# Reading a 64 MiB input at another row pitch: seven blocks at 448 KiB and one at 64 KiB, in place of eight at 512 KiB

## The chip, the cores and the metric

The kernel runs on one core of a Trainium2 chip. The metric is the time of one execution on the device in microseconds (us), as the median of several runs. All runs told of here are fast (granted clock 1.000, nothing disturbed). The input lies in HBM, the chip's main memory; DMA engines copy it in packets to the on-chip memory, whose 128 rows are called partitions. A transfer has *landed* when all its packets have arrived and the waiting engine may go on. The span that a profile shows is 1.7 to 1.8 us shorter than the time of the same run.

## The reference

```python
x = np.random.randn(32, 512, 1024).astype(np.float32)      # 64 MiB
multiplier = 0.5
def reference(x, multiplier):
    return (np.sum(x, axis=-1) * multiplier).astype(np.float32)   # [32, 512]
```

There are 16384 rows of 1024 numbers (4 KiB each). Each row becomes one number, and no row depends on another: any row may lie on any partition, as long as its sum is stored in the right place.

## The kernel before

The 16384 rows are dealt to 128 partitions, 128 consecutive rows each. A block is 16 rows of every partition (8 MiB), there are eight blocks, and three buffers. Seven blocks are loaded by one DMA each and split between two engines: VectorE reduces eight rows by one instruction, ScalarE takes eight by one activation each.

```python
x_flat = x.flatten_outer_dims()
N, D = x_flat.shape
rows = N // P                                   # 128 rows per partition
x_rows = x_flat.rearrange("(p c) d -> p c d", p=P)
out_view = out.rearrange("b s -> (b s)").rearrange("(p c) -> p c", p=P)
B = 16
n_blocks = rows // B                            # 8
x_pool = ctx.enter_context(tc.tile_pool(name="x", bufs=3))
# ... (cut)
for b in range(n_blocks - 1):
    c0 = b * B
    t = x_pool.tile([P, B, D], fp32, name="xb")
    loads.append(nc.sync.dma_start(out=t, in_=x_rows[:, c0 : c0 + B, :]))
    h = B // 2
    nc.vector.reduce_sum(out=sums[:, c0 : c0 + h], in_=t[:, 0:h, :], axis=mybir.AxisListType.X)
    # ... (cut: the multiplication by 0.5)
    for r in range(h, B):
        act_row(t, r, c0 + r)                   # ScalarE, one row of all partitions
# ... (cut) the last block comes in five DMAs, of 8, 5, 2 rows, 640 and 384 columns of the last row,
# so that little is left to compute after the last of them; its sums go out by a store of their own
nc.sync.dma_start(out=out_view[:, 0:c1], in_=res[:, 0:c1])        # 56 KB
# ... (cut)
store = nc.sync.dma_start(out=out_view[:, c1:], in_=res[:, c1:])  # 8 KB, the end of the kernel
```

A step from one partition to the next is 128 rows in HBM: a pitch of 512 KiB, for all eight blocks.

## Time and profile before

| | |
|---|---|
| time | 162.91 us (162.87 to 163.31, 3 runs) |
| span of the profiled run | 160.9 us |
| share of the DMA queue in 16 engines' span | 97.2% |
| VectorE, ScalarE busy | 42%, 42% |
| a steady packet of x (64 KiB, one partition's 16 rows) | 2.418 us |
| landing of the last piece of x but one, on which the chain waits | 157.43 us, taken up at 157.46 us |
| landing of the last piece (192 KB) | 157.91 us |

These lines are from the page of the kernel before: the span, the busy tenths of the DMA engines in 40 slices, the DMA queues (packets, MB, share of 16 engines), the chain that ended last by engine, and the two costliest groups (busy us and mean ns of one; then idle us before them and what ended it).

```profile
span 160.9 us, 236 instructions
...
DMA  7997997998998998998998998998998998999991
...
q1 hardware_dynamic: 2016, 67.18, 97.2%
q14 instruction: 1, 0.01, 0.0%
...
DMA 86%; DVE 11%; SPq 1%; issue 0%; DVEq 0%
...
L50 ACT ACTIVATE xb<-xb 128x1024 f32<-128x1024 f32 x63 | 65.6, 1043 | 88.2 <-DMA xb<-in_x_dram 88.2
L76 DVE TENSOR_REDUCE sums<-xb 128x8 f32<-128x8192 f32 x7 | 60.8, 8686 | 85.0 <-DMA xb<-in_x_dram 85.0
```

Both computing engines stand idle for more than half of the span, nearly all of it waiting for x. The one queue of loads and stores keeps the 16 engines busy for 97.2% of the span.

The next lines are the stage table of the kernel before: stretch in us, its length, busy time of the engines, then clock, DMA share and GB/s.

```profile
core 0: us, DVE busy (x) ACT busy (x) POOL busy (x), PEclk, DMA share, GB/s
22.00:41.50 19.50, 8.86 (x2) 8.42 (x16) 0.00 (x0) 1.00 0.99 430
41.50:60.90 19.40, 8.86 (x2) 8.42 (x16) 0.00 (x0) 1.00 1.00 432
...
80.20:99.60 19.40, 8.86 (x2) 8.42 (x16) 0.00 (x0) 1.00 1.00 433
```

And these are pieces of its chain of waits (start, length, what). The pieces between them are a wait for a buffer (a VectorE reduction) and issues.

```profile
0.43 41.13 DMA xb<-in_x_dram
...
50.36 49.27 DMA xb<-in_x_dram
...
109.78 47.66 DMA xb<-in_x_dram
...
157.46 0.49 DVE xb L60
...
158.04 0.42 DVE xb L60
```

The DMA share is 0.99 to 1.00 while blocks stream in. The chain steps over a reduction of 8.7 us twice only because a load waits there for its buffer; two more blocks are queued at that time, so the engines don't run dry. From 157.46 us, when the last piece but one has landed, two short VectorE operations and a store remain, 3.4 us in all; the last piece lands during the first of them. (The prediction's "last landing" is the 157.46 us.)

Last, the start of the first five reductions on VectorE, from the timeline (start, length, ..., idle before and what ended it). Each starts when its block has landed on all partitions, so this is a clock of the load stream.

```profile
22.26 8.69 DVE L76 TENSOR_REDUCE sums<-xb 128x8 f32<-128x8192 f32 x1 [22.26 <-DMA xb<-in_x_dram]
41.59 8.69 DVE L76 TENSOR_REDUCE sums<-xb 128x8 f32<-128x8192 f32 x1 [10.43 <-DMA xb<-in_x_dram]
60.94 8.69 DVE L76 TENSOR_REDUCE sums<-xb 128x8 f32<-128x8192 f32 x1 [10.46 <-DMA xb<-in_x_dram]
80.29 8.69 DVE L76 TENSOR_REDUCE sums<-xb 128x8 f32<-128x8192 f32 x1 [10.46 <-DMA xb<-in_x_dram]
99.65 8.69 DVE L76 TENSOR_REDUCE sums<-xb 128x8 f32<-128x8192 f32 x1 [10.47 <-DMA xb<-in_x_dram]
```

A block takes 19.33 to 19.36 us: eight packets of 2.42 us on each engine. The first one comes at 22.26 us.

### The profile page before, as it was taken

What the parts mean: (1) busy time and instruction counts of PE and PEld (TensorE: products, weight loads), DVE (VectorE), ACT (ScalarE), POOL (GpSimd) and SP (SyncE); (2) the same over time, 40 slices, a digit from 0 to 9 for tenths busy, and PEclk for the clock granted to TensorE, in tenths of its full rate; (3) what the DMA queues carried; (4) which work ended last, traced back from release to release, by engine and by line L of the source; (5) the groups of instructions that cost most, each with busy time, mean ns of one, the idle gap of its engine ahead of it and who ended that gap; (6) DMA issues with size and microseconds to landing.
All of it is one profiled execution on the core that took longest, in us unless ns stands there. A gap on an engine that the chain in (4) does not pass through costs nothing.

```text
span 160.9 us, 236 instructions
## 1 busy us (share of the span) xinstructions
DVE 68.1 (42%) x34; ACT 67.8 (42%) x127; POOL 0.2 (0%) x4
## 2 busy tenths in 40 slices
DVE  0000049700695008930099102990049700597453
ACT  3000049600694008920099001980039700596952
POOL 0000000000000000000000000000000000000000
DMA  7997997998998998998998998998998998999991
GB/s 261 522 440 342 522 440 342 522 424 359 522 424 359 522 424 359 522 424 359 522 424 361 522 407 375 522 407 375 522 407 375 522 407 375 407 448 396 425 386 40
DMA packets 2017, 67.18 MB, mean 418 GB/s; under 512 B 480, under 2 KB 608, under 8 KB 736
## 3 DMA queue, kind: packets, MB, share of 16 engines
q1 hardware_dynamic: 2016, 67.18, 97.2%
q14 instruction: 1, 0.01, 0.0%
HBM read 67.11 MB, written 0.07 MB: 418 GB/s over the span
## 4 chain that ended last, share of the span: by engine, by line
DMA 86%; DVE 11%; SPq 1%; issue 0%; DVEq 0%
DMA xb<-in_x_dram 86%; DVE sums L76 11%; SPq L94 1%; DVE xb L60 1%; SPq L74 0%; DVE part L60 0%; DVEq L190 0%
## 5 line engine op out<-in xcount | busy, mean ns | idle before, releaser
L50 ACT ACTIVATE xb<-xb 128x1024 f32<-128x1024 f32 x63 | 65.6, 1043 | 88.2 <-DMA xb<-in_x_dram 88.2
L76 DVE TENSOR_REDUCE sums<-xb 128x8 f32<-128x8192 f32 x7 | 60.8, 8686 | 85.0 <-DMA xb<-in_x_dram 85.0
L50 ACT ACTIVATION_READ_ACCUMULATOR xb<-xb 128x1 f32 x63 | 11.8, 187 | 0.0
L60 DVE CUSTOM_DVE_ANT_0 xb<-xb 128x512 f32<-128x512 f32 (+1 forms) x9 | 5.6, 667 | 5.1 <-DMA xb<-in_x_dram 4.9
L50 ACT ACT_TABLE_LOAD x1 | 1.3, 1283 | 1.7 <-PEq L176 1.7
L79 DVE TENSOR_SCALAR res<-sums 128x8 f32<-128x8 f32 x7 | 1.2, 172 | 0.2
L60 DVE DVE_READ_ACCUMULATOR2_ANT res<- 128x1 f32 x9 | 0.7, 83 | 0.0
L60 DVE CUSTOM_DVE_ANT_0 xb<-xb,part 128x192 f32<-128x192 f32 x1 | 0.4, 419 | 0.1
L176 POOL MEMSET const-uint8-127<- 128x1 uint8 x1 | 0.1, 103 | 0.0
L176 POOL MEMSET const-bfloat16-1.0<- 128x1 bf16 x1 | 0.1, 102 | 0.0
L176 POOL MEMSET const-float32-0.0<- 128x1 f32 x1 | 0.1, 99 | 0.2 <-issue 0.2
L176 POOL MEMSET const-float32-1.0<- 128x1 f32 x1 | 0.1, 99 | 0.0
L60 DVE DVE_READ_ACCUMULATOR2_ANT part<- 128x1 f32 x1 | 0.1, 83 | 0.0
## 6 DMA issues: line engine op xcount, KB each, us to landing
xb<-in_x_dram SPq DMA_DIRECT2D x1, 4096.0 KB, 39.6
xb<-in_x_dram SPq DMA_DIRECT2D x1, 2560.0 KB, 45.4
xb<-in_x_dram SPq DMA_DIRECT2D x1, 1024.0 KB, 47.4
xb<-in_x_dram SPq DMA_DIRECT2D x1, 320.0 KB, 47.7
xb<-in_x_dram SPq DMA_DIRECT2D x1, 192.0 KB, 47.6
xb<-in_x_dram SPq DMA_DIRECT2D x7, 49.3
out_dram<-res SPq DMA_DIRECT2D x1, 56.0 KB, 10.8
out_dram<-res SPq DMA_DIRECT2D x1, 8.0 KB, 1.4
```

Source lines behind the costliest of these rows:

```text
L50: acts.append(nc.scalar.activation(out=t[:, r, :], in_=t[:, r, :], func=mybir.ActivationFunctionType.Copy, scale=mul, accum_out=res[:, col ...
L60: nc.vector.tensor_tensor_reduce(out=t[:, r, lo:mid], in0=t[:, r, lo:mid], in1=t[:, r, mid:hi], scale=mul, scalar=start, op0=ADD, op1=ADD, ...
L76: nc.vector.reduce_sum(out=sums[:, c0 : c0 + h], in_=t[:, 0:h, :], axis=mybir.AxisListType.X)
L79: nc.vector.tensor_single_scalar(out=res[:, c0 : c0 + h], in_=sums[:, c0 : c0 + h], scalar=mul, op=mybir.AluOpType.mult,)
L94: nc.sync.dma_start(out=t[:, lo:hi, :], in_=x_rows[:, c0 + lo : c0 + hi, :])
L176: nc = _bacc.Bacc("TRN2", target_bir_lowering=False, num_devices=1)
```

## The change

The intent: take the large power of two out of the addresses that the 128 partitions read side by side. Seven blocks form one region in which a partition's rows are 112 rows apart (448 KiB); the last block forms a region of its own, 16 rows apart (64 KiB, so the 8 MiB are contiguous). The sums of each region then are contiguous in the output too.

```diff
-    x_rows = x_flat.rearrange("(p c) d -> p c d", p=P)
-    out_view = out.rearrange("b s -> (b s)").rearrange("(p c) -> p c", p=P)
+    out_flat = out.rearrange("b s -> (b s)")
...
+    own = rows - B                              # 112
+    x_rows = x_flat[0 : P * own, :].rearrange("(p c) d -> p c d", p=P)
+    x_last = x_flat[P * own : N, :].rearrange("(p c) d -> p c d", p=P)
+    out_rows = out_flat[0 : P * own].rearrange("(p c) -> p c", p=P)
+    out_last = out_flat[P * own : N].rearrange("(p c) -> p c", p=P)
...   # the five loads of the last block
-                out=t[:, lo:hi, :], in_=x_rows[:, c0 + lo : c0 + hi, :]
+                out=t[:, lo:hi, :], in_=x_last[:, lo:hi, :]
...
-    nc.sync.dma_start(out=out_view[:, 0:c1], in_=res[:, 0:c1])
+    nc.sync.dma_start(out=out_rows, in_=res[:, 0:own])
...
-    store = nc.sync.dma_start(out=out_view[:, c1:], in_=res[:, c1:])
+    store = nc.sync.dma_start(out=out_last, in_=res[:, own:])
```

The instructions on all engines are the same in number, order and shape; only addresses in HBM differ.

More of the change, by code (lines that the diff above doesn't have):

```diff
@@ L100 @@
             nc.sync.dma_start(
-                out=t[:, B - 1, lo:hi], in_=x_rows[:, c0 + B - 1, lo:hi]
+                out=t[:, B - 1, lo:hi], in_=x_last[:, B - 1, lo:hi]
             )
         )
-    c1 = c0
-    nc.sync.dma_start(out=out_view[:, 0:c1], in_=res[:, 0:c1])
+    nc.sync.dma_start(out=out_rows, in_=res[:, 0:own])
     on_act = {4, 5, 6, 7, 11, 12, 14}
```

## The prediction

> **What bounds the kernel.** The transfers from HBM, and not by HBM but by the 16 DMA engines themselves. The page gives the hardware queue 97.2% of 16 engines' span; VectorE and ScalarE are busy 42% each and wait for x (groups of instructions: 85.0 us and 88.2 us of idle time, released by the DMA). The chain of waits is 86% DMA of x. Its 11% of `sums` reduction is only the wait of a buffer's next load, while two blocks are already queued: the stage table shows the DMA share at 0.99 to 1.00 from 22 to 119 us (430 to 435 GB/s). So everything up to the last landing at 157.5 us is the load stream; the remaining 3.4 us are two short VectorE operations, the last 8 KB store (1.4 us to landing) and the end.
>
> **The packet records.** A packet is 64 KiB, one partition's 16 rows. In the steady part nearly every one takes 2.418 to 2.420 us (27.1 GB/s per engine, 434 GB/s for 16), without spread. The Trainium skill, "DMA: Bandwidth & Descriptors", section Bandwidth, puts the ceiling of the 16 SBUF ports at 435.2 GB/s; the trace agrees within 0.5%. The same page, section Latency and other measured facts, gives 207 GB/s at a row pitch of 512 KiB against 214 for a padded pitch, in copies from HBM to HBM. This trace shows no such loss: at 512 KiB the engines already run at their ceiling.
>
> **What the change does.** Nothing is removed or added: same 12 loads, two stores, bytes, tiles and engine work. Seven blocks are read at a pitch of 448 KiB in place of 512 KiB, the last at 64 KiB, each still as contiguous runs of 64 KiB.
> - Steady packets: no gain; 64 packets' worth per engine at 2.42 us stay 154.8 us.
> - First block: its packets have a mean of 2.515 us against 2.420; the excess is 8 x 0.095 = about 0.8 us per engine, nearly all in each engine's first packet (3.0 to 3.5 us). I take it for the fill of the stream; were it pitch conflicts, 0.8 us is the most that could come back. I allow 0.1 us.
> - First store (56 KB): runs of 448 B, now adjacent instead of 512 B apart; its packets (25 ns, eight per engine) end the stream beside the computing. Nothing.
> - Last store, on the critical path: 128 runs of 64 B, 512 B apart before, adjacent now (8 KB contiguous). If runs merge, or neighbouring partial writes collide, its 1.4 us may move by 0.2 us either way.
>
> **Prediction: 162.8 us**, 8 in 10 from 162.2 to 163.5. Faster by over 2%: 0.02; within 2%: 0.96; slower by over 2%: 0.02.
>
> **What would show it.** Right: steady packets stay at 2.42 us, last landing of x at 157 to 158 us, same order of waits, tail of 3.2 to 3.6 us. Conflicts that matter: first-block packets near 2.42 us and the last landing 0.5 us or more earlier. A bad new pitch: packets over 2.5 us in the first seven blocks (448 KiB) or only in the last (64 KiB), and the DMA share below 1.00 or GB/s below 430 in those stages.
>
> **What would make it wrong.** Several of the 16 engines meeting in one part of HBM at one of the new pitches, so that it and not the engine sets the packet's time; fewer engines for the now contiguous stores; or sessions that differ by more than the 0.3% seen in three runs.

## The result, and the profile after

| | before | after |
|---|---|---|
| time, median (lowest to highest) | 163.01 us (162.87 to 163.31, 6 runs) | 162.59 us (162.52 to 162.73, 6 runs) |
| ratio, 95% interval | | 0.9973 (0.9960 to 0.9986) |

A ratio here is the mean time of one kernel's fast runs over the mean of the other's fast runs of the same rounds, so it isn't quite the ratio of the medians. The time is inside the predicted range and within 2%, as predicted. But the two sets of runs don't overlap: there is a small gain, 0.42 us between the medians, where 0.1 us had been allowed for. The range is 1.3 us wide, three times the gain, so that the time alone says little about the reasoning behind it. The six runs of before were also 0.1 us slower in the median than the 162.91 us from which the prediction was reckoned, and this hides a part of the miss.

The lines of the page, the stage table and the chain of the kernel after, as above:

```profile
span 160.8 us, 236 instructions
...
DMA  7996996996996996996996996996996996998990
...
q1 hardware_dynamic: 2016, 67.18, 97.3%
q14 instruction: 1, 0.01, 0.0%
...
DMA 86%; DVE 11%; SPq 1%; issue 0%; DVEq 0%
...
L55 ACT ACTIVATE xb<-xb 128x1024 f32<-128x1024 f32 x63 | 65.6, 1042 | 88.2 <-DMA xb<-in_x_dram 88.2
L81 DVE TENSOR_REDUCE sums<-xb 128x8 f32<-128x8192 f32 x7 | 60.8, 8686 | 85.0 <-DMA xb<-in_x_dram 85.0
```

```profile
core 0: us, DVE busy (x) ACT busy (x) POOL busy (x), PEclk, DMA share, GB/s
22.00:41.50 19.50, 9.01 (x3) 8.57 (x17) 0.00 (x0) 1.00 0.99 430
41.50:60.90 19.40, 8.91 (x3) 8.47 (x17) 0.00 (x0) 1.00 1.00 432
...
80.20:99.60 19.40, 8.62 (x2) 8.28 (x16) 0.00 (x0) 1.00 1.00 433
```

```profile
0.43 40.80 DMA xb<-in_x_dram
...
50.03 49.57 DMA xb<-in_x_dram
...
109.71 47.74 DMA xb<-in_x_dram
...
157.47 0.49 DVE xb L65
...
158.02 0.42 DVE xb L65
```

Nothing has moved: the stages have the same GB/s, and the last piece of x but one is taken up at 157.47 us in place of 157.46 (the last lands at 157.89 in place of 157.91). The profiled run of before took 162.63 us, less than any of its six timed runs, and so these two profiles can't show the gain by their ends. The clock of the load stream says more (start of the first five reductions, after):

```profile
21.91 8.69 DVE L81 TENSOR_REDUCE sums<-xb 128x8 f32<-128x8192 f32 x1 [21.91 <-DMA xb<-in_x_dram]
41.26 8.69 DVE L81 TENSOR_REDUCE sums<-xb 128x8 f32<-128x8192 f32 x1 [10.46 <-DMA xb<-in_x_dram]
60.61 8.69 DVE L81 TENSOR_REDUCE sums<-xb 128x8 f32<-128x8192 f32 x1 [10.46 <-DMA xb<-in_x_dram]
79.97 8.69 DVE L81 TENSOR_REDUCE sums<-xb 128x8 f32<-128x8192 f32 x1 [10.46 <-DMA xb<-in_x_dram]
99.62 8.69 DVE L81 TENSOR_REDUCE sums<-xb 128x8 f32<-128x8192 f32 x1 [10.77 <-DMA xb<-in_x_dram]
```

After is 0.35 us ahead at the first block (21.91 against 22.26), and keeps 0.32 to 0.35 us until the fourth. Then it loses them in one step: from the fourth to the fifth block it takes 19.65 us, before 19.36. The records of single packets name both steps. They are no view of the page, so they are given here in words and as a table worked out from them. (A record doesn't name its engine; a packet is counted to the engine whose packet ends where it starts.)

```
                                                      before     after
start of the 16 engines' first packets, us        1.01..1.91   1.00..1.55   (mean 1.38 / 1.13)
first packets, mean duration, us                       3.18         3.20
end of the first packets, mean (latest), us      4.56 (4.99)  4.33 (4.65)
later 64 KiB packets, starting after 5 us: mean       2.4203       2.4202
packet of the instruction queue: start, length  86.40, 0.31  83.97, 0.31
x packet just behind it: start, length          86.70, 2.72  84.28, 2.78
last engine done with block 4 / block 5, us     79.90, 99.23  79.51, 99.14
```

(Block 4 and block 5 count from one.) In both kernels one DMA engine has to fetch 8 KiB of instructions in between. That takes 0.31 us, and the engine's next packet takes 2.72 or 2.78 us by the record instead of 2.42: in sum it falls behind by 0.61 us in before and 0.67 us in after. In the profiled run of before this engine had been 0.75 us ahead of the last one and stayed 0.14 us ahead of it, so the last landing didn't move. In the profiled run of after it had been only 0.37 us ahead, and became the last one by 0.30 us. So the theory to test: the new pitch lets the engines start earlier, by a quarter of a microsecond on average and more for the latest of them; and the fetch took nearly all of it back in this pair of profiles.

### The profile page after: what moved, and what is told of

The parts are those of the page before. It is cut to its first block, busy times and chain, and to the rows that moved or that the text cites. A ratio compares the mean times of both kernels' runs of the same rounds, so it can differ in the third digit from the quotient of the medians.

```text
span 160.8 us, 236 instructions
## 1 busy us (share of the span) xinstructions
DVE 68.1 (42%) x34; ACT 67.9 (42%) x127; POOL 0.2 (0%) x4
## 4 chain that ended last, share of the span: by engine, by line
DMA 86%; DVE 11%; SPq 1%; issue 0%; DVEq 0%
DMA xb<-in_x_dram 86%; DVE sums L81 11%; SPq L99 1%; DVE xb L65 1%; SPq L79 0%; DVE part L65 0%; DVEq L194 0%
```

## The experiments

The rivals: (1) *start*: the pitch acts on the first packets, through the seven blocks' 448 KiB; (2) *tail*: the last block's 64 KiB pitch is what helps; (3) *stores*: the contiguous last store helps; (4) *scatter*: there is no gain, builds and runs just differ. Twelve kernels were run, in three sessions on three chips, each kernel with five or six runs, the kernel before among them each time (162.84 us, 9 runs; 163.05 us, 11 runs; 162.93 us, 11 runs). Seven give a wrong result on purpose, because loads and stores no longer belong together or rows are read twice.

### First session: is it real, and is it loads or stores?

`null_before` is the program of before with a comment added:

```diff
+    # the same program again
     nc = tc.nc
```

> The program of before with a comment added. If the 0.27% (0.42 us) of the change is scatter between builds or executions, this too differs from before by some 0.2 to 0.5 us, either way. If the 0.42 us is real, this gives 163.0 us and a ratio within 0.999 to 1.001 whose interval holds 1.

Measured: 162.89 us (162.76 to 162.99), ratio 1.0002 (0.9990 to 1.0015). Correct. A build by itself makes no difference.

`after_again` is the changed kernel, unchanged:

```diff
 (no edit to the kernel after)
```

> The changed kernel again, on another chip session. If the gain is real: 162.6 us, ratio 0.9965 to 0.998, interval clear of 1. If it was scatter: a ratio of 1 within the interval.

Measured: 162.65 us (162.59 to 162.72), ratio 0.9987 (0.9975 to 1.0000). Correct. The kernel repeats its time to 0.06 us, but before was quicker on this chip (162.84 us), so the gain is half as large, 0.19 us, and the interval only just touches 1. Less than was expected.

`new_loads_old_stores` has the loads of after and the stores of before:

```diff
-    out_rows = out_flat[0 : P * own].rearrange("(p c) -> p c", p=P)
-    out_last = out_flat[P * own : N].rearrange("(p c) -> p c", p=P)
+    out_view = out_flat.rearrange("(p c) -> p c", p=P)
+    out_rows, out_last = out_view[:, 0:own], out_view[:, own:]
```

> Loads at the new pitches, stores at the old ones; the result is wrong on purpose (rows land in other places). Load theory: the gain comes from how the load stream starts or ends at the new pitches, so this has all of it, 162.6 us. Store theory: the gain comes from the last 8 KB store being one contiguous run, so this has none of it, 163.0 us. In the profile: load theory has the last landing of x 0.3 us or more earlier after the engines' first starts are counted; store theory has it unchanged.

Measured: 162.61 us (162.45 to 162.87), ratio 0.9982 (0.9969 to 0.9996). In its profile the last packet of x ends at 157.79 us, later than in `null_before` (157.65 us), so the expectation of an earlier landing failed; the fetch had made its engine the last (the fifth reduction starts 19.74 us after the fourth). But the first reduction starts at 22.03 us against 22.36 us in `null_before` of the same session.

`old_loads_new_stores` is the reverse:

```diff
-    x_rows = x_flat[0 : P * own, :].rearrange("(p c) d -> p c d", p=P)
-    x_last = x_flat[P * own : N, :].rearrange("(p c) d -> p c d", p=P)
+    x_all = x_flat.rearrange("(p c) d -> p c d", p=P)
+    x_rows, x_last = x_all[:, 0:own, :], x_all[:, own:, :]
```

> Loads at a pitch of 512 KiB throughout, stores contiguous as in the changed kernel; the result is wrong on purpose. Store theory: 162.6 us, all of the gain, with the last store's issue to the end of the span 0.2 us or more shorter. Load theory: 163.0 us, ratio 1 within 0.001.

Measured: 162.91 us (162.68 to 163.01), ratio 1.0001 (0.9988 to 1.0013). The store theory falls, and with both null results the scatter theory too: what gain there is comes with the loads.

### Second session: which loads, and can the place in HBM set the pace at all?

`only_448` (against after; stores as before):

```diff
-    x_last = x_flat[P * own : N, :].rearrange("(p c) d -> p c d", p=P)
+    x_last = x_flat.rearrange("(p c) d -> p c d", p=P)[:, own:, :]
...   # and the stores as in new_loads_old_stores
```

> First seven blocks at 448 KiB, last block and stores as before (wrong on purpose). So far the kernels with the new loads have their engines' first packets end at 4.29 to 4.33 us on average, those with 512 KiB at 4.51 to 4.57 us. Start theory (the pitch acts in the first packets alone): 4.3 us here, first reduction starting at 21.6 to 22.0 us in place of 22.3, and all of the gain, 0.2 to 0.4 us off the whole time. Tail theory (the last block's 64 KiB pitch is what helps): no gain.

Measured: 162.58 us (162.51 to 162.89), ratio 0.9978 (0.9965 to 0.9991). First packets end at 4.31 us on average, and the first reduction starts at 21.91 us. All of the gain.

`only_last_64` (against after; stores as before):

```diff
-    x_rows = x_flat[0 : P * own, :].rearrange("(p c) d -> p c d", p=P)
+    x_rows = x_flat.rearrange("(p c) d -> p c d", p=P)
...   # and the stores as in new_loads_old_stores
```

> First seven blocks at 512 KiB, last block at 64 KiB, stores as before (wrong on purpose). Start theory: no gain, ratio 1 within 0.001, first packets end at 4.5 us on average. Tail theory: the gain of 0.2 to 0.4 us.

Measured: 163.06 us (162.97 to 163.23), ratio 1.0005 (0.9993 to 1.0017). First packets end at 4.58 us. The tail theory falls. Its profile showed something not looked for, in the starts of its reductions:

```profile
22.35 8.69 DVE L81 TENSOR_REDUCE sums<-xb 128x8 f32<-128x8192 f32 x1 [22.35 <-DMA xb<-in_x_dram]
41.68 8.69 DVE L81 TENSOR_REDUCE sums<-xb 128x8 f32<-128x8192 f32 x1 [10.43 <-DMA xb<-in_x_dram]
61.36 8.69 DVE L81 TENSOR_REDUCE sums<-xb 128x8 f32<-128x8192 f32 x1 [10.80 <-DMA xb<-in_x_dram]
```

The third block takes 19.68 us instead of 19.35. In the packet records, eight packets of that block, all starting between 50.2 and 51.0 us, take 2.7 to 2.9 us. The instruction queue had nothing then. So at 512 KiB the later packets are not always free of disturbance, as the one profile of before had suggested.

`first_508` (against before) moves only the first block, to a pitch of 127 rows:

```diff
+    x_first = x_flat[0 : P * (rows - 1), :].rearrange("(p c) d -> p c d", p=P)
-        loads.append(nc.sync.dma_start(out=t, in_=x_rows[:, c0 : c0 + B, :]))
+        loads.append(nc.sync.dma_start(out=t, in_=(x_first if b == 0 else x_rows)[:, c0 : c0 + B, :]))
```

> Only the first block's pitch is changed, from 128 to 127 rows (508 KiB); the other seven stay at 512 KiB (wrong on purpose). Start theory, with the power of two as the cause: first packets end at 4.3 us on average and 0.2 to 0.4 us are gained, as with 448 KiB. Rival, that the gain is spread over all blocks (each block a little): an eighth of the gain, not to be told from 0. Rival, that any multiple of 64 KiB or less matters rather than the power of two: between.

Measured: 162.80 us (162.65 to 163.70), ratio 0.9997 (0.9979 to 1.0014). Inconclusive. One of six runs took 163.70 us and carries the mean; the median is 0.25 us below that of before. In the profile, one only, the start is nearly as early as at 448 KiB: first packets end at 4.40 us, the first reduction starts at 22.06 us.

`pitch_0` (against before) lets every partition read the same rows:

```diff
-    x_rows = x_flat.rearrange("(p c) d -> p c d", p=P)
+    x_rows = x_flat.rearrange("(p c) d -> p c d", p=P)[0:1].broadcast_to([P, N // P, D])
```

> Every partition reads the same rows (pitch 0, wrong on purpose), so the 16 engines read the same 64 KiB of HBM together in each step: the most crowded pattern that can be written. Engine theory (each engine sets the packet's time): steady packets stay at 2.42 us and the time within 0.5 us of before. HBM theory (the place in HBM can set it): packets of 3 us or more and a time above 180 us; then the 2.42 us at 512 KiB says that this pitch is merely not crowded enough.

Measured: 163.09 us (162.49 to 163.16), ratio 0.9999 (0.9987 to 1.0012). The queue's line of its page:

```profile
core 0 of [0], span 161.4 us
...
q1 hardware_dynamic: 2016, 67.18, 97.0%
```

Even with all 16 engines on the same 64 KiB the median packet takes 2.418 us. The engine theory holds for the pace. Two smaller effects cancel: the first packets end sooner than in any other kernel (4.13 us on average; they start later, at 1.60 us, but take only 2.54 us), and 35 later packets take over 2.5 us, the fetch's not counted, 30 of them in the second and third block. This is one crowded pattern, not all of them: different rows that meet in one part of HBM may behave otherwise than equal ones.

### Third session: the first block alone, the power of two, and the fetch

`first_448` (against before) is `first_508` with 112 rows:

```diff
+    x_first = x_flat[0 : P * (rows - 16), :].rearrange("(p c) d -> p c d", p=P)
```

> Only the first block at 448 KiB, the other seven at 512 KiB (wrong on purpose). Start theory: the whole gain of 0.2 to 0.45 us, first reduction starting at about 21.9 us in place of 22.3, first packets ending at 4.3 us on average. Rival, that the later blocks share in the gain: less than half of it, under 0.15 us.

Measured: 162.59 us (162.51 to 163.31), ratio 0.9986 (0.9972 to 1.0001). The first reduction starts at 21.85 us, first packets end at 4.38 us. Five of six runs (162.51 to 162.75) lie below all eleven of before in the session (from 162.78), and the median is 0.34 us lower; one run of 163.31 us is slower than all of them, and brings the interval to 1. So the first block's pitch alone is enough for the earlier start. That it is enough for the gain is likely from the medians, but not settled by the interval; one run in six was without it.

`all_64` (against before) makes every block one contiguous run of 8 MiB:

```diff
+    x_blk = x_flat.rearrange("(b p c) d -> b p c d", p=P, c=16)
+    out_blk = out.rearrange("b s -> (b s)").rearrange("(b p c) -> p b c", p=P, c=16)
-        loads.append(nc.sync.dma_start(out=t, in_=x_rows[:, c0 : c0 + B, :]))
+        loads.append(nc.sync.dma_start(out=t, in_=x_blk[b]))
...   # the last block's loads and the two stores accordingly
```

> Every block is one contiguous run of 8 MiB, pitch 64 KiB; correct. Start theory with the power of two as the cause: 64 KiB is one as well, so first packets end at 4.5 us and nothing is gained, 163.0 us. Start theory with the distance between engines as the cause (the nearer, the sooner, as pitch 0 gave 4.13 us): 4.2 to 4.3 us and 0.2 to 0.5 us gained, if the later packets stay at 2.42 us.

Measured: 162.81 us (162.57 to 162.87), ratio 0.9990 (0.9977 to 1.0003). Correct. Its stream starts as early as at 448 KiB (first packets end at 4.31 us, first reduction at 21.87 us), and no packet but the fetch's takes over 2.5 us. So a power of two as such does not delay the start: 64 KiB is one as well. That only large ones do, 512 KiB among them, is not excluded. In time the gain is unclear, and less than the start promises; in its profile the fetch again fell on an engine that became the last (the fifth reduction starts 19.78 us after the fourth). Nor is the pitch all that this edit changes: the first store now consists of 896 packets of 64 B in place of 128 of 448 B. The last x packet ends at 157.48 us (after: 157.44), but the last piece lands at 158.04 us (after: 157.89). So the time of `all_64` is no clean measure of the pitch.

`few_act_old` (against before) and `few_act_new` (against after) are the same edit. It gives VectorE 14 of 16 rows in the first six blocks, so ScalarE has 27 activations in place of 63:

```diff
-        h = B // 2
+        h = B // 2 if b == n_blocks - 2 else 14
```

> Before, with 14 of 16 rows of the first six blocks on VectorE, so that ScalarE has 27 activations in place of 63; correct, pitch of 512 KiB. All traces so far show one 8 KiB packet of the instruction queue at 84 to 87 us, and most a single x packet of 2.7 to 2.8 us beside it. Fetch theory: one DMA engine then falls 0.3 us behind, and what the runs of one kernel differ by is whether it is a late or an early one; with fewer ScalarE instructions the fetch is gone, the runs lie closer together, and the time is 0 to 0.3 us less. Rival, that the fetch does no harm: the same time as before within 0.1 us and the same spread.

Measured: 162.95 us (162.70 to 163.25), ratio 1.0001 (0.9989 to 1.0013). Correct. No gain and no smaller spread. Its profile has no fetch at 84 to 87 us (it came at 159.2 us, behind the last landing), but 23 packets over 2.5 us, spread over blocks two to five and one in the seventh: slow packets as in `only_last_64` took the place of the fetch. The smaller spread that the fetch theory expected did not come.

> The changed kernel with the same shift of rows to VectorE; correct. If the earlier start (0.3 us) and the absent fetch (0.3 us at the engine that has it) add: 162.2 to 162.4 us, last landing of x at 157.1 us in place of 157.4, and the two kernels here differ by more than the profiles of before and after did, by 0.3 us. If they don't add: 162.6 us as the change alone.

Measured: 162.30 us (162.21 to 162.50), ratio 0.9963 (0.9951 to 0.9975). Correct. The fetch came at 158.5 us, and no packet after the first ones takes over 2.5 us. The starts of three of its reductions:

```profile
21.85 15.09 DVE L81 TENSOR_REDUCE sums<-xb 128x14 f32<-128x14336 f32 x1 [21.85 <-DMA xb<-in_x_dram]
...
79.88 15.09 DVE L81 TENSOR_REDUCE sums<-xb 128x14 f32<-128x14336 f32 x1 [4.05 <-DMA xb<-in_x_dram]
99.23 15.09 DVE L81 TENSOR_REDUCE sums<-xb 128x14 f32<-128x14336 f32 x1 [4.06 <-DMA xb<-in_x_dram]
```

From the fourth to the fifth block it takes 19.35 us, where after took 19.65. The last piece of x but one is taken up at 157.16 us by the timeline, 0.3 us before the two main kernels. All its runs lie below all timed runs of before in all sessions, and below all eleven of after (162.52 and up); but after ran in other sessions, and the intervals of their ratios to before overlap (0.9951 to 0.9975, and 0.9960 to 0.9986 or 0.9975 to 1.0000). It clearly beats before; that it beats after is likely, not settled.

### All traces side by side

Worked out from the packet records and the timelines; one profiled run each. "Over 2.5 us" counts 64 KiB packets that start after 5 us, without the one behind the fetch.

```
kernel                 pitch of block 1   first packets end,  first reduction  packets over
                       / of blocks 2-7     mean, us            starts, us       2.5 us
before                 512 / 512           4.56                22.26             0
null_before            512 / 512           4.51                22.36             5
old_loads_new_stores   512 / 512           4.57                22.35             2
only_last_64           512 / 512           4.58                22.35            15
few_act_old            512 / 512           4.47                22.31            23
first_508              508 / 512           4.40                22.06             2
first_448              448 / 512           4.38                21.85             0
after                  448 / 448           4.33                21.91             0
after_again            448 / 448           4.29                21.80             0
new_loads_old_stores   448 / 448           4.33                22.03             0
only_448               448 / 448           4.31                21.91             0
few_act_new            448 / 448           4.31                21.85             0
all_64                  64 / 64            4.31                21.87             0
pitch_0                  0 / 0             4.13                21.90            35
```

The column of first reductions follows the pitch of the first block without exception: 22.26 to 22.36 us at 512 KiB, 21.80 to 22.03 us at 448 KiB. The last column follows the pitch of the later blocks: at 448 or 64 KiB none in six traces, at 512 KiB some in five of seven (in `null_before` all five of them in the first block, which has 512 KiB there too). What in HBM, or on the way to it, delays the engines at 512 KiB was not shown by any run; neither a power of two as small as 64 KiB nor crowding on one place (pitch 0) does it at the start.

The traces also show why an earlier start is not a gain of the same size. In `before`, `null_before` and `old_loads_new_stores` the engine that has the fetch was 0.68 to 0.75 us ahead of the last one, fell behind by 0.55 to 0.62 us, and still was not the last: from the fourth to the fifth block it takes 19.32 to 19.38 us. In the seven traces with an earlier start, a fetch in the stream and at most two slow packets (`first_508`, `first_448`, `after`, `after_again`, `new_loads_old_stores`, `only_448`, `all_64`) the engines lie closer together (first to last 0.42 to 0.76 us, against 0.82 to 0.90 us in the three); the engine with the fetch was only 0.26 to 0.46 us ahead, fell behind by 0.60 to 0.67 us and became the last each time: 19.61 to 19.79 us. (`only_last_64` and `pitch_0`, with many slow packets, lie between: 19.48 and 19.53 us.) So the first reduction starts 0.41 us earlier on average at 448 KiB (22.33 us in the five traces all at 512 KiB in blocks 1 to 7, 21.91 us in the four at 448 KiB with a fetch in the stream), and 0.19 us of that is left when the last piece but one is taken up (157.71 and 157.52 us). This fits both `few_act` results: without the fetch, 512 KiB gained nothing and 448 KiB gained 0.3 us. It is read from one profile each; no run put the fetch on a chosen engine.

## Why the prediction was right, and where it was off

- **What bounds the kernel: right.** The pace is that of the DMA engines: 2.418 us for a median packet at pitches of 512, 448, 64 and 0 KiB. The Trainium skill, "DMA: Bandwidth & Descriptors", section Bandwidth, puts the ceiling of the SBUF ports at 435.2 GB/s; 16 engines at 64 KiB in 2.418 us make 433.7. With no room there, a change of addresses could not bring 2%.
- **The page's loss at 512 KiB: right that it doesn't apply in full.** The same page's section Latency and other measured facts gives 207 GB/s at 512 KiB against 214 at full rate (a padded pitch of 4 MiB), 3%, for copies within HBM. Here, with reads from HBM into SBUF, 512 KiB costs 0.19 to 0.47 us of 163 over the kernels that read all seven blocks at 448 KiB with nothing else changed in the computing, 0.1 to 0.3%. The measurement decides: the loss is there, more than ten times smaller, and not in the steady packet (2.418 us at every pitch tried).
- **"First block ... I allow 0.1 us": the term that was mis-sized.** It measured 0.35 us in the pair of profiles (22.26 to 21.91 us). The prediction summed the durations of packets and took their excess of 0.8 us for all that could be won. In this pair the durations of the first packets did not change (3.18 and 3.20 us); their starts did, 1.38 us on average to 1.13, and 1.91 to 1.55 for the latest. The start times were in the trace before, but a single trace could not tell what another pitch would give. Over all traces it is the same on average (512 KiB: starts 1.46, durations 3.07 us in five traces; 448 KiB in all seven blocks: 1.18 and 3.13 us in five), but not in each: `first_448` starts at 1.34 us with durations of 3.04 us. The end of the first packets is the steadier witness.
- **"This trace shows no such loss": true of that trace, too wide as a conclusion.** Of the six other traces with later blocks at 512 KiB, `first_508` and `first_448` included, five have 2 to 23 slow packets. In `only_last_64` one group of them made a block 0.33 us late. The time of before lies scattered over 162.67 to 163.31 us in all sessions, that of after over 162.52 to 162.73.
- **Stores: right.** `old_loads_new_stores` has a ratio of 1.0001; the last store takes 1.4 us to land in both main kernels.
- **Tail and last landing: right, the landing by luck.** 157.47 us, with 3.4 us after it. But the last landing was no good witness of the gain: an instruction fetch on one engine, of which the prediction says nothing, took back 0.30 of the 0.35 us by which the stream had started earlier.

Left open: how much of the difference in time comes from the start and how much from the absent slow packets (`first_448` changes the first block alone, and got 0.34 us in the median, 0.14% in the mean); what slowed the timed runs of before, all of which took longer than its profiled run of 162.63 us; and the cause of both within HBM.

## What to carry to other kernels

Here the median packet took 2.418 us at all four pitches, so the layout in HBM could not make the stream's pace faster; what it still changed was when the engines got going and, by the traces, how often they were disturbed, tenths of a microsecond. The first reduction started 17.27 us (before) and 17.26 us (after) after the latest of the first packets had ended. So look at the spread of the engines' first packets and at odd packets from other queues on one of them, not at mean durations alone. And a tighter start left less room for a disturbance: the fetch that cost nothing in three traces with the engines 0.82 to 0.90 us apart cost 0.26 to 0.44 us of a block's 19.35 in seven with the engines 0.42 to 0.76 us apart. And for effects of this size one pair of profiles proves nothing: use several timed runs, a null build, and a clock inside the trace such as the start of each block's first instruction.

## What the Trainium skill lacked or had wrong

- "DMA: Bandwidth & Descriptors", section Latency and other measured facts, HBM row pitch: it has copies from HBM to HBM only. For reads into SBUF by one core the steady packet is the same at pitches of 512, 448, 64 and 0 KiB (median 2.418 us). What 512 KiB costs is a later start (first packets end at 4.47 to 4.58 us on average, against 4.29 to 4.33 with all seven blocks at 448 KiB) and single slow packets (0 to 23 of some 865).
- The same row doesn't say where the large powers of two begin. Here 64 KiB starts as early as 448 KiB (first packets end at 4.31 us), and 508 KiB, which is none, nearly so (4.40 us with the first block alone changed; 4.38 us at 448 KiB in the same way).
- "DMA: Bandwidth & Descriptors", section Queues, rings and completion order, mentions refills on the runtime's queue row; neither it nor another page says what one costs a load stream on the same DMA engine: 8 KiB take 0.31 us, and the x packet behind them on that engine takes 2.66 to 2.78 us in twelve traces, in place of 2.42, so that the engine falls 0.55 to 0.67 us behind. It came at 84 to 87 us with 63 activations on ScalarE, and at 158.5 or 159.2 us, behind the loads, with 27.
- "HBM Reference", section Specifications, gives about 425 GB/s for a core that streams alone; here five stages of 19 us each show 430 to 435 GB/s, and the whole span of before, with its start and end, 418 GB/s.
